# Split weight buffers four instead of three, raw ones eleven instead of thirteen, and the one-hot token columns by eight compares

## The chip, the cores and the metric

The kernel runs on one core of a Trainium2 chip. What counts is the time of one execution on the device, in microseconds (us); of several runs the median is taken. A profile is one execution recorded instruction by instruction. Its engines are TensorE (PE, with its weight loads as PEld), VectorE (DVE), ScalarE (ACT), GpSimd (POOL) and SyncE (SP, which here only issues DMAs). Work reaches an engine in the order of its own queue; engines wait for one another through semaphores.

## The reference, cut to what matters

One layer of a backbone over 1024 latent tokens of width 1024: a normalised input is projected, goes through a long convolution and a gated recurrence, is projected back and added to x. Then comes the part that the change touches, a mixture of 16 experts in which each expert chooses its 128 tokens:

```
aff = softmax(h @ router_w)                      # 1024 x 16
gates, idx = top_k(aff.T, cap)                   # cap = 2 * 1024 / 16 = 128 tokens for each expert
xg = h[idx]                                      # 128 x 1024 per expert
y  = (silu(xg @ w1[e]) * (xg @ w3[e])) @ w2[e]   # w1, w3: 1024 x 2048, w2: 2048 x 1024
out = zeros.at[idx].add(y * gates)               # back to the tokens
```

The result is scaled, added to x and normalised. All is float32.

## The kernel before, in words

The matrix products keep float32 accuracy by splitting each operand into a high half (a rounded copy) and a low half (the rest): `mm3` (L63) makes three matmuls, high by high, high by low, low by high.

The expert weights, 402 MB, are read once, in 384 pieces of 1 MB (128 partitions x 2048 float32). Each expert is worked in two halves of 1024 hidden columns, `i` in 0 to 31. A half takes four pieces of w1, four of w3 and then, for the half before it, four of w2 (`order`, L977). A piece goes through these stages:

- `fetch(n)` (L986) issues its load, on SP's queue, into a buffer `raw`. There are NA = 8 of these in one pool and NB = 5 in another, used in turn. The first eight pieces are loaded during the output projection, by POOL (`stored`, L1035), the next five by POOL right after it (L1112).
- `split(n)` (L1212) copies `raw` to `ehi` on ACT (L1217) and subtracts it into `elo` on DVE (L1223). There are NHI = 3 buffers of each. The first three low halves are made by POOL instead (L1221). When the low half is done the `raw` buffer is free for another load.
- `take()` (L1243) hands the next split piece to PE and, just before, orders the split and the load of later ones: `split(at + NHI - 1)` and `fetch(at + NHI - 1 + NA + NB)`. With that, up to NHI + NA + NB = 16 pieces are loaded or on their way.
- PE multiplies it: 12 matmuls of 128x512 per piece, into `pa` (w1, w3) or `pb` (w2).

Between these stand the other jobs of a half: `sa` is the activation, on ACT (L1280) and DVE (L1282); it is transposed by PE (L1316) and split again into `hh` by ACT (L1318) and DVE (L1319). Once per expert the result is scaled on DVE (L1305) and added to the tokens in memory by an indirect DMA of POOL (L1310). Also once per expert, two experts ahead, `gather(e)` (L1179) finds the tokens: `posT` holds for each token its place (1 to 128) in the expert's list, `iot` the numbers 1 to 128; comparing them gives one-hot columns `oh`, and 16 small matmuls with token numbers give the list `idx`, by which POOL loads the rows `xg` (L1191). `transposed` (L1194) turns these to `hcT`, by PE, ACT (`hf`, L1207, and L1208) and DVE (L1209).

The program is written in one order, but a planner lays out each engine's queue by costs and due times of its own, so that for instance the transposes of one half stand among the matmuls of the next. `issue_after` (`after`, L1022) keeps an instruction behind another.

Ahead of the experts come the output projection and the routing (L1083, t = 0 to 9), the search for each expert's threshold in ten rounds (L1128, which use the tables `jcol` and `rmat`), the places `posT` (L1169), the first two gathers and 9 matmuls that nobody reads (`idle`, L1257). The tables `rmat` and `jcol` are loaded into the pool `late`, which opens at L888. The pool `tp` (L1006) lies where the arena of the stages before was, which closes at L958.

Of the kernel before, what the change touches and what calls it, by code (L numbers as in the profile page):

```python
# [11 lines left out]
F32 = mybir.dt.float32  # L12
F32R = mybir.dt.float32r
BF16 = mybir.dt.bfloat16
# [4 lines left out]
ALU = mybir.AluOpType  # L19
# [3 lines left out]
P = 128  # L23
# [4 lines left out]
NE = 16  # L28
# [29 lines left out]
def kernel(ctx: ExitStack, tc: tile.TileContext, T: dict, out: bass.AP, dbg=None, stop=None):  # L58
    nc = tc.nc
    V, S, PE, G = nc.vector, nc.scalar, nc.tensor, nc.gpsimd  # L60
# [7 lines left out]
    def f32(a):  # L68
        return a.bitcast(F32)

    def brow(src, off, n):

        return bass.AP(tensor=src.tensor, offset=src.offset + off, ap=[[0, P], [1, n]])
# [4 lines left out]
    def bank(tag, bufs, shape=(P, 512), dtype=F32):  # L78
        return ps.tile(list(shape), dtype, tag=tag, bufs=bufs, name=tag)
# [25 lines left out]
    pad = lambda pool, n: pool.tile([P, n], F32, name="pad")  # L105
# [550 lines left out]
    if True:  # L656
# [4 lines left out]
        for hd in range(4):  # L661
# [71 lines left out]
            for dr in range(2):  # L733
                seq = [8, 9] + list(range(7)) if dr == 0 else [9, 8] + list(range(7, 0, -1))
                prev = None
                for b in range(3):
# [9 lines left out]
                    for i, c in enumerate(grp):  # L746
                        n = 3 * b + i
# [139 lines left out]

    late = ctx.enter_context(tc.tile_pool(name="late", bufs=1))  # L888
    aff = late.tile([P, 8, NE], F32, name="aff")
    posT = late.tile([P, 8, NE], BF16, name="posT")  # L890
    iot = late.tile([P, P], BF16, name="iot")
    nc.gpsimd.dma_start(iot, T["iota"])
    tok = late.tile([P, 8, 2], BF16, name="tok")
    nc.gpsimd.dma_start(tok, T["tok"])
    pad(late, 40)
    rmat = late.tile([P, 3, P], BF16, name="rmat")
    nc.gpsimd.dma_start(rmat, T["rmat"])
    jcol = late.tile([P, 10], F32, name="jcol")
    nc.scalar.dma_start(jcol, T["jcol"])
    octx = ctx.enter_context(ExitStack())  # L900
    op = octx.enter_context(tc.tile_pool(name="op", bufs=1))
    pad(op, 112)
# [70 lines left out]


    NS = 2 * NE
    NA, NB, NHI = 8, 5, 3
    order = []  # L977
    for i in range(NS + 1):
        if i < NS:
# [6 lines left out]
    def fetch(n, eng=nc.sync):  # L986


        last = n - NP
        if last < 5:  # L990
            nm, i, j = order[n] if last < 0 else ("x", 0, last)
            e, fc = divmod(i, 2)
            if last == 4:
                src = brow(T["final_g"], 0, D).rearrange("p (a n) -> p a n", a=1)
            elif nm == "x":
                src = xacc[2 * j * P:2 * (j + 1) * P, :].rearrange("(c p) n -> p c n", p=P)
            elif nm == "exp_w2":
                src = T[nm][e].rearrange("(q c p) n -> q p c n", p=P, c=2)[4 * fc + j]
            else:
                src = T[nm][e].rearrange("(k p) f -> p k f", p=P)[:, 2 * j:2 * j + 2, fc * 1024:(fc + 1) * 1024]  # L1000
            early = n % (NA + NB) < NA
            raws[n] = (ew if early else eb).tile([P, 2048], F32, name="raw", bufs=NA if early else NB)
            return eng.dma_start(raws[n].rearrange("p (a b) -> p a b", b=1024)[:, 0:src.shape[1], :], src)

    tctx = ctx.enter_context(ExitStack())
    tp = tctx.enter_context(tc.tile_pool(name="tp", bufs=1, side="right"))  # L1006
    R = tp.tile([P, L], F32, name="R")


    rwg = tp.tile([P, 8, 32], F32, name="rwg")  # L1010
# [11 lines left out]
    def after(ins):  # L1022
        return tc.issue_after(ins.ins if hasattr(ins, "ins") else ins)
# [49 lines left out]
    def rows8(t):  # L1073
        h2, st = tl[t]["h2"], tl[t]["st"]
        pa = bank("pb", 2)
        PE.transpose(pa[:, 0:P], tl[t]["a8"].rearrange("p e j -> p (e j)"), ident)
        tl[t]["row"] = S.copy(R[:, t * P:(t + 1) * P], pa[:, 0:P])
        V.tensor_copy(aff[:, t, :], tl[t]["a8"][:, :, 0])
# [49 lines left out]
    for r in range(10):  # L1128
        V.tensor_scalar(junk, R, thr.bitcast(F32), None, ALU.is_ge, ALU.add, accum_out=cnt)
        V.tensor_scalar(ind, cnt, float(CAP), None, ALU.is_ge)  # L1130
# [48 lines left out]
    def gather(e):  # L1179

        oh = ep.tile([P, 8, P], BF16, name="oh", bufs=1)
        V.tensor_tensor(oh, iot[:].unsqueeze(1).broadcast_to([P, 8, P]), posT[:, :, e:e + 1].broadcast_to([P, 8, P]), ALU.is_equal)
        pi = bank("pt", 2)
        for a in range(8):
            for i in range(2):
                PE.matmul(pi[:, 0:1], oh[:, a, :], tok[:, a, i:i + 1], start=(a + i == 0), stop=(a + i == 8))
        idx = ep.tile([P, 1], I32, name="idx", bufs=4)
        f_ = V.tensor_copy(idx, pi[:, 0:1])
        found[0] = found[0] or f_
        xg = ep.tile([P, D + NE], F32, name="xg", bufs=3)  # L1190
        G.indirect_dma_start(xg[:], None, h2d[:], bass.IndirectOffsetOnAxis(ap=idx[:, 0:1], axis=0))  # L1191
        return idx, xg

    def transposed(e, xg):  # L1194
        xT = [a[:, :, e % 2 * P:(e % 2 + 1) * P] for a in hcT]
        for b in range(2):
            pt = bank("pt", 2)
            hf = ep.tile([P, 4, P], F32, name="hf", bufs=2)
            for c in range(4):
                k = 4 * b + c  # L1200
                PE.transpose(pt[:, c * P:(c + 1) * P], xg[:, k * P:(k + 1) * P], ident)
            for c in range(4):
                k = 4 * b + c
                if e == 0 and b == 1:
                    V.tensor_scalar(hf[:, c, :], pt[:, c * P:(c + 1) * P], gs2[:, k:k + 1], mod2[:, k, 0:1], ALU.mult, ALU.add)
                else:
                    S.activation(hf[:, c, :], pt[:, c * P:(c + 1) * P], AF.Identity, scale=gs2[:, k:k + 1], bias=mod2[:, k, 0:1])  # L1207
            S.copy(xT[0][:, 4 * b:4 * b + 4, :], hf)  # L1208
            V.tensor_tensor(xT[1][:, 4 * b:4 * b + 4, :], hf, f32(xT[0][:, 4 * b:4 * b + 4, :]), ALU.subtract)  # L1209
        return xT  # L1210

    def split(n):  # L1212
        if n < NP:
            raw = raws.pop(n)
            hi = eb.tile([P, 2048], F32R, name="ehi", bufs=NHI)
            with after(tl[7]["row"]):
                S.copy(hi, raw)  # L1217
            lo = eb.tile([P, 2048], F32R, name="elo", bufs=NHI)
            if n < NHI:
                with after(pieces[-1]):  # L1220
                    pieces.append(G.tensor_tensor(lo, raw, f32(hi[:]), ALU.subtract))  # L1221
            else:
                V.tensor_tensor(lo, raw, f32(hi[:]), ALU.subtract)  # L1223
            parts[n] = [t.rearrange("p (a b) -> p a b", b=1024) for t in (hi, lo)]
# [18 lines left out]
    def take():  # L1243
        nonlocal at
        if at > 0:
            split(at + NHI - 1)
            fetch(at + NHI - 1 + NA + NB)
        at += 1
        return parts.pop(at - 1)

    for n in range(NHI):
        split(n)
        fetch(n + NA + NB)
    g = {0: gather(0)}
    g[1] = gather(1)

    idle = bank("pb", 2)  # L1257
    for _ in range(9):
        PE.matmul(idle[:, 0:P], ident, ident, start=True, stop=True)
    xTs = {0: transposed(0, g[0][1])}  # L1260
    py = None
    hs_ = {}
    for i in range(NS + 1):
        e, fc = divmod(i, 2)
# [46 lines left out]
        if i < NS:  # L1311
            hh = [ep.tile([P, 8, P], F32R, name=f"hh{i_}") for i_ in range(2)]
            for b in range(2):
                pt = bank("pt", 2)
                for c in range(4):
                    PE.transpose(pt[:, c * P:(c + 1) * P], sa[:, b, c * P:(c + 1) * P], ident)  # L1316
                pv = pt.rearrange("p (c t) -> p c t", t=P)
                S.copy(hh[0][:, 4 * b:4 * b + 4, :], pv)  # L1318
                V.tensor_tensor(hh[1][:, 4 * b:4 * b + 4, :], pv, f32(hh[0][:, 4 * b:4 * b + 4, :]), ALU.subtract)  # L1319
            hs_[i] = hh  # L1320
            if fc == 0:
                if e + 2 < NE:
                    g[e + 2] = gather(e + 2)
                if e + 1 < NE:
                    xTs[e + 1] = transposed(e + 1, g[e + 1][1])
# [152 lines left out]
```

## Time and profile before

| | |
|---|---|
| runs shown | 2187.92, 2191.95, 2196.3 us; median 2191.95 |
| profiled execution | 2189.24 us, of which the span from first to last instruction 2186.7 |
| PE | 2048.9 us busy, 94% of the span |
| DVE | 1733.5 us, 79% |
| ACT | 1242.2 us, 57% |
| POOL | 201.7 us, 9% |
| low halves `elo` on DVE (L1223) | 863.3 us in 381 |
| high halves `ehi` on ACT (L1217) | 732.8 us in 384 |
| DMA | 565.94 MB, mean 259 GB/s |

A busy PE is not a PE at its peak: matmuls overlap, and their ends are modelled (398 ns stand for one, while they start closer together). So lost time is read from the starts, or from what the weight loads wait for. Idle time of an engine that is not the bottleneck costs nothing. In a row of waits the engine and line that waited stand first, then what ended the wait; the releaser is inferred.

### The profile page before, as it was taken

The numbers are of one execution on the slowest core, as the hardware profiler recorded it, in microseconds if no ns is written. First come the engines' busy times: TensorE is split into PE (matmuls) and PEld (weight loads), VectorE is DVE, ScalarE is ACT, GpSimd is POOL, SyncE is SP. The second block draws the span as 40 slices with busy tenths as digits, with TensorE's granted clock in tenths as the row PEclk, the third lists the DMA queues.
The fourth block names the chain that finished last, engine by engine and source line by source line (L and its number), as shares of the span: only waits on it lengthen the run. The fifth ranks groups of instructions, "written<-read, shape, count | busy, mean of one in ns | idle before, by whom it ended". The sixth has DMA issues, their size and how long they took to land.

```text
span 2186.7 us, 30384 instructions
## 1 busy us (share of the span) xinstructions
PE 2048.9 (94%) x11761; PEld 1621.4 (74%) x11761; DVE 1733.5 (79%) x2051; ACT 1242.2 (57%) x1461; POOL 201.7 (9%) x234
## 2 busy tenths in 40 slices
PE   7987899799999998894999999999999999999997
PEld 2444788788788786773888888787877878787775
DVE  6778356746778887666899999888988889888887
ACT  3566235333542212142877777777777777777774
POOL 1121100100000002124000000000000000100000
PEclk9998999899999999996999999999999999999999
DMA  7874521320234327476999999999999999999992
GB/s 246 271 260 149 159 64 54 108 83 21 64 112 144 111 88 256 141 256 248 343 372 379 397 387 369 358 384 373 381 363 360 387 381 362 364 381 375 352 332 120
DMA packets 185404, 565.94 MB, mean 259 GB/s; under 512 B 15545, under 2 KB 26380, under 8 KB 185261
## 3 DMA queue, kind: packets, MB, share of 16 engines
q1 hardware_dynamic: 147044, 478.41, 58.9%
q0 software_dynamic: 28784, 76.46, 11.5%
q10 hardware_dynamic: 9432, 9.15, 1.3%
q8 instruction: 92, 1.51, 0.3%
q14 instruction: 52, 0.42, 0.1%
HBM read 522.59 MB, written 41.50 MB: 258 GB/s over the span
## 4 chain that ended last, share of the span: by engine, by line
PE 76%; DVE 9%; issue 5%; DMA 5%; ACT 4%; POOL 1%; DVEq 0%; ACTq 0%; SPq 0%; POOLq 0%
PE pa L65 15%; PE pa L66 15%; PE pa L64 14%; PE pb L66 5%; PE pb L65 5%; PE pb L64 5%; PE pt L864 2%; PE pb L845 2%; DVE elo L1223 2%; PE pf L546 2%; ACT ehi L1217 2%; PE pt L1316 1%; DVE arena L727 1%; DVE arena L725 1%; DMA oraw<-in_w_out 1%
## 5 line engine op out<-in xcount | busy, mean ns | idle before, releaser
L1223 DVE TENSOR_TENSOR elo<-raw,ehi 128x2048 fp32r<-128x2048 f32 x381 | 863.3, 2289 | 103.3 <-ACT ehi L1217 99.4
L1217 ACT CAST ehi<-raw 128x2048 fp32r<-128x2048 f32 x384 | 732.8, 1917 | 213.6 <-PE pb L66 93.8
L65 PE MATMUL pa<-elo,hcT 128*128 128x512 f32 x1024 | 407.6, 398 | 14.7 <-DVE elo L1223 14.6
L66 PE MATMUL pa<-ehi,hcT 128*128 128x512 f32 x1024 | 401.6, 392 | 0.0
L64 PE MATMUL pa<-ehi,hcT 128*128 128x512 f32 x1024 | 377.0, 392 | 2.0 <-ACT hcT L1208 1.4
L65 PEld LDWEIGHTS pa<-elo,hcT 128*128 128x128 f32 x1024 | 193.0, 188 | 72.5 <-DVE elo L1223 34.3
L64 PEld LDWEIGHTS pa<-ehi,hcT 128*128 128x128 f32 x1024 | 192.9, 189 | 42.5 <-ACT hcT L1208 1.8
L66 PEld LDWEIGHTS pa<-ehi,hcT 128*128 128x128 f32 x1024 | 193.2, 189 | 37.5
L65 PE MATMUL pb<-elo,hh 128*128 128x512 f32 x512 | 204.9, 400 | 0.0
L66 PE MATMUL pb<-ehi,hh 128*128 128x512 f32 x512 | 200.0, 391 | 0.4 <-DVE hh L1319 0.4
L64 PE MATMUL pb<-ehi,hh 128*128 128x512 f32 x512 | 184.6, 390 | 0.4 <-ACT hh L1318 0.4
L66 PE MATMUL pa<-hT,wlo 128*128 128x512 f32 x448 | 177.6, 397 | 0.5 <-DVE wlo L580 0.5
L64 PE MATMUL pa<-hT,whi 128*128 128x512 f32 x448 | 177.9, 397 | 0.0
L65 PE MATMUL pa<-hT,whi 128*128 128x512 f32 x448 | 175.8, 393 | 0.0
L1310 POOL DMA_INDIRECT xacc<-xg,idx x15 | 45.4, 3024 | 846.2 <-DVE xg L1305 846.2
L64 PEld LDWEIGHTS pb<-ehi,hh 128*128 128x128 f32 x512 | 96.1, 188 | 21.6 <-ACT hh L1318 0.9
L65 PEld LDWEIGHTS pb<-elo,hh 128*128 128x128 f32 x512 | 96.1, 188 | 21.5
L66 PEld LDWEIGHTS pb<-ehi,hh 128*128 128x128 f32 x512 | 96.2, 188 | 18.8 <-DVE hh L1319 0.9
L66 PEld LDWEIGHTS pa<-hT,wlo 128*128 128x128 f32 x448 | 84.1, 188 | 18.7 <-DVE wlo L580 1.4
L65 PEld LDWEIGHTS pa<-hT,whi 128*128 128x128 f32 x448 | 84.2, 188 | 16.9 <-issue 0.2
L64 PEld LDWEIGHTS pa<-hT,whi 128*128 128x128 f32 x448 | 84.2, 188 | 16.8 <-issue 0.2
L546 PE MATMUL pf<-Yh,mt 128*128 128x256 f32 x256 | 73.8, 421 | 16.8 <-ACT he L552 5.9
(407 smaller groups left out, 3112.1 us busy)
## 6 DMA issues: line engine op xcount, KB each, us to landing
raw<-in_exp_w SPq DMA_DIRECT2D x371, 1024.0 KB, 7.7
aw<-in_ada_w SPq DMA_DIRECT2D x96, 256.0 KB, 4.9
wraw<-in_w_in SPq DMA_DIRECT2D x64, 256.0 KB, 3.3
raw<-in_exp_w POOLq DMA_DIRECT2D x13, 1024.0 KB, 8.3
mt<-in_fwm POOLq DMA_DIRECT2D x64, 128.0 KB, 3.6
Hd<-he ACTq DMA_DIRECT2D x32, 256.0 KB, 4.4
wod<-arena POOLq DMA_DIRECT2D x32, 256.0 KB, 3.5
arena<-in_fwm SPq DMA_DIRECT2D x32, 256.0 KB, 7.6
```

The costliest lines, as they stand in the source:

```text
L64: PE.matmul(ps, lhs[0], rhs[0], start=first, stop=False)
L65: PE.matmul(ps, lhs[0], rhs[1], start=False, stop=False)
L66: PE.matmul(ps, lhs[1], rhs[0], start=False, stop=last)
L546: PE.matmul(pt[:, :HC], mt[:, i, :], Y[:, 2 * n + i, :], start=(i == 0), stop=(i == 1))
L725: V.tensor_tensor(kv, kv, view(F2, h, [[2 * h, nb], [LT - h, 2], [0, h]]), ALU.mult)
L727: V.tensor_tensor(qv, qv, view(F2, LT + h, [[2 * h, nq], [-(LT + h), 2], [0, h]]), ALU.mult)
L845: PE.matmul(px[:, j, :], fm[:, j, i, :], Y[:, 2 * n + i, :], start=(i == 0), stop=(i == 1))
L864: PE.matmul(pz[:, j, :], im[:, i, j, :], pp[:, i, :], start=(i == 0), stop=(i == 1))
L1217: S.copy(hi, raw)
L1223: V.tensor_tensor(lo, raw, f32(hi[:]), ALU.subtract)
L1310: G.indirect_dma_start(xacc[:], bass.IndirectOffsetOnAxis(ap=idx[:, 0:1], axis=0), xg[:, 0:D], None, compute_op=ALU.add)
L1316: PE.transpose(pt[:, c * P:(c + 1) * P], sa[:, b, c * P:(c + 1) * P], ident)
```

## The change

The raw buffers of the second pool go from 5 to 3 (11 in all) and the split pairs from 3 to 4. In bytes the pool stays the same: two raw buffers are 16 KB per partition, one split pair as well. The look-ahead goes from 16 pieces to 15. The first three splits stay with POOL; the fourth is ordered after the first expert's tokens are transposed, with ACT and DVE.

The compare of `iot` with `posT`, one instruction over 128x1024 with two broadcast inputs, becomes eight over 128x128, each with a column of `posT` as a scalar operand. For that `posT` becomes float32. The tables `rmat` and `jcol` move from `late` to `tp`, and so their loads come later in the program.

```
-    posT = late.tile([P, 8, NE], BF16, name="posT")
+    posT = late.tile([P, 8, NE], F32, name="posT")
...
-    pad(late, 40)
-    rmat = late.tile([P, 3, P], BF16, name="rmat")
-    nc.gpsimd.dma_start(rmat, T["rmat"])
-    jcol = late.tile([P, 10], F32, name="jcol")
-    nc.scalar.dma_start(jcol, T["jcol"])
+    pad(late, 50)
...
-    NA, NB, NHI = 8, 5, 3
+    NA, NB, NHI = 8, 3, 4
...
     R = tp.tile([P, L], F32, name="R")
+    rmat = tp.tile([P, 3, P], BF16, name="rmat")
+    nc.gpsimd.dma_start(rmat, T["rmat"])
+    jcol = tp.tile([P, 10], F32, name="jcol")
+    nc.scalar.dma_start(jcol, T["jcol"])
...
         oh = ep.tile([P, 8, P], BF16, name="oh", bufs=1)
-        V.tensor_tensor(oh, iot[:].unsqueeze(1).broadcast_to([P, 8, P]), posT[:, :, e:e + 1].broadcast_to([P, 8, P]), ALU.is_equal)
+        for a in range(8):
+            V.tensor_scalar(oh[:, a, :], iot, posT[:, a, e:e + 1], None, ALU.is_equal)
...
-            if n < NHI:
+            if n < 3:
                 with after(pieces[-1]):
                     pieces.append(G.tensor_tensor(lo, raw, f32(hi[:]), ALU.subtract))
...
-    for n in range(NHI):
+    for n in range(3):
         split(n)
         fetch(n + NA + NB)
...
     xTs = {0: transposed(0, g[0][1])}
+    for n in range(3, NHI):
+        split(n)
+        fetch(n + NA + NB)
```

## Rows read from the trace of the kernel before

**Rows 1.** The page: busy us of each engine (share of the span), instructions.
```profile
PE 2048.9 (94%) x11761; PEld 1621.4 (74%) x11761; DVE 1733.5 (79%) x2051; ACT 1242.2 (57%) x1461; POOL 201.7 (9%) x234
```
**Rows 2.** Waits, 1030 to 2190 us: who <- released by: us in total, times, longest.
```profile
ACT ehi L1217 <- PE pb L66: 93.8, 91, 1.6
...
PEld pa L65 <- DVE elo L1223: 34.3, 60, 2.0
```
**Rows 3.** Groups of instructions, 1050 to 2190 us: busy us, mean ns, idle before.
```profile
L1223 DVE TENSOR_TENSOR elo<-raw,ehi 128x2048 fp32r<-128x2048 f32 x377 | 854.2, 2289 | 95.1 <-ACT ehi L1217 91.2
L1217 ACT CAST ehi<-raw 128x2048 fp32r<-128x2048 f32 x376 | 717.9, 1918 | 207.7 <-PE pb L66 93.8 <-PE pa L66 82.9 <-DVE sa L1282 24.2
```
**Rows 4.** Timeline of PE about 1519 us: start us, us, instruction.
```profile
1519.31 0.39 PE L66 MATMUL pa<-ehi,hcT 128*128 128x512 f32 x1
...
1519.99 0.39 PE L66 MATMUL pa<-ehi,hcT 128*128 128x512 f32 x1
```
**Rows 5.** Waits of the weight loads, 1140 to 1340, then 1340 to 2060 us.
```profile
PEld pa L65 <- DVE elo L1223: 0.4, 2, 0.2
...
PEld pa L65 <- DVE elo L1223: 27.4, 50, 2.0
PEld L1186 <- DVE hh L1319: 2.5, 9, 0.3
```
**Rows 6.** Timeline of DVE about four compares, four experts.
```profile
1201.73 1.22 DVE L1182 TENSOR_TENSOR oh<-iot,posT 128x1024 bf16<-128x1024 bf16 x1
...
1270.25 1.22 DVE L1182 TENSOR_TENSOR oh<-iot,posT 128x1024 bf16<-128x1024 bf16 x1
...
1477.79 1.22 DVE L1182 TENSOR_TENSOR oh<-iot,posT 128x1024 bf16<-128x1024 bf16 x1
...
1546.16 2.29 DVE L1223 TENSOR_TENSOR elo<-raw,ehi 128x2048 fp32r<-128x2048 f32 x1
1548.37 1.22 DVE L1182 TENSOR_TENSOR oh<-iot,posT 128x1024 bf16<-128x1024 bf16 x1
```
**Rows 7.** Two windows: length, PE, PEld, DVE, ACT, POOL busy, clock, DMA share, GB/s.
```profile
1140.00:1340.00 200.00, 200.00 (x960) 165.46 (x958) 181.82 (x110) 154.08 (x121) 10.57 (x6) 1.00 1.00 381
1340.00:2060.00 720.00, 708.18 (x3312) 572.99 (x3312) 637.46 (x385) 540.42 (x428) 53.07 (x20) 1.00 0.99 372
```
**Rows 8.** Waits of SP's queue from 900 us, and the page's DMA issues.
```profile
SPq L1003 <- DVE elo L1223: 943.2, 370, 27.6
...
raw<-in_exp_w SPq DMA_DIRECT2D x371, 1024.0 KB, 7.7
```
**Rows 9.** PE's timeline about 2045 us, and the window behind it.
```profile
2044.55 0.39 PE L66 MATMUL pa<-ehi,hcT 128*128 128x512 f32 x1
...
2047.79 0.80 PE L65 MATMUL pa<-elo,hcT 128*128 128x512 f32 x1 [1.59 <-DVE elo L1223]
...
2048.00:2051.00 3.00, 3.00 (x8) 2.33 (x9) 3.00 (x3) 1.53 (x1) 0.00 (x0) 0.51 0.98 358
```
**Rows 10.** Waits of the weight loads, 1030 to 1140, then 2060 to 2160 us.
```profile
PEld pa L65 <- DVE elo L1223: 1.4, 3, 0.7
...
PEld pa L65 <- DVE elo L1223: 5.2, 5, 1.4
PEld pb L66 <- DVE hh L1319: 0.9, 1, 0.9
```
**Rows 11.** A window at the start of the experts, columns as in rows 7.
```profile
1030.00:1040.00 10.00, 9.97 (x36) 8.11 (x37) 4.12 (x4) 4.43 (x3) 0.00 (x0) 0.81 0.01 2
```
**Rows 12.** DVE's timeline at 2125 us, and the instructions of L1130.
```profile
2125.37 1.66 DVE L1268 TENSOR_SCALAR hcT<-iot,idf 128x128 fp32r<-128x128 bf16 x8
...
L1130 DVE TENSOR_SCALAR ind<-cnt x10: 146/150/157, 994.5 to 1013.0; 128x1 bf16<-128x1 f32 x10
```
**Rows 13.** Timelines of PE and of DVE ahead of the first gather.
```profile
1016.67 3.88 PE L1259 MATMUL pb<-ident 128*128 128x128 f32 x18
...
1017.51 1.23 DVE L1182 TENSOR_TENSOR oh<-iot,posT 128x1024 bf16<-128x1024 bf16 x1
```
**Rows 14.** Timelines of POOL and of ACT where the arena comes free.
```profile
937.21 0.57 POOL L1036 DMA_DIRECT2D xacc<-oxt  x1 [10.04 <-DVE oxt L1029]
...
930.96 0.63 ACT L1033 ACTIVATE oh<-oxt 128x512 f32<-128x512 f32 x1 [0.87 <-DVE oxt L1029]
```

## The prediction

> **What bounds the kernel now.** I read the page's busy times first: TensorE (PE) 94% of the span, VectorE (DVE) 79% [rows 1]. In the expert stage, the second half of the span, the DMA engines are full too (a share of 0.99 to 1.00 [rows 7]), so three things could set its pace. The waits between 1030 and 2190 us tell them apart. PE waits for one thing that counts: the low half of a split weight piece, `elo`, written by DVE at L1223. Its weight loads sat idle 34.3 us in 60 such waits. ScalarE (ACT) in turn waits for PE before it may write the high half `ehi`, 93.8 us behind the matmuls into `pb` alone: the three pairs of split buffers are all in use [rows 2]. That is a ring: PE frees a pair, ACT fills `ehi` (1.92 us), DVE fills `elo` (2.29 us) [rows 3], 4.2 us in a row, while PE has two pieces left, each 12 matmuls at about 0.227 us (1519.31 to 1519.99 is three) [rows 4], so 5.4 us. The slack is 1.2 us, and any other instruction of that length on ACT or DVE ahead of a split shows on PE.
>
> Whether it does varies along the stage. From 1140 to 1340 us PE lost 0.4 us to `elo`; from 1340 to 2060 us it lost 27.4 [rows 5]. The one-hot compare, once per expert, stood 68.5 us apart in the first stretch (1201.73 to 1270.25) and 70.6 in the second (1477.79 to 1548.37) [rows 6]. So an expert costs PE 68.5 us where nothing holds it, and that is the floor that I use. DVE was 91% busy in the fast stretch (181.8 of 200) and 89% in the slow one, so it is not DVE's throughput, but the order of its work and the short ring [rows 7].
>
> Loads are not the bound. The DMA queue waits for split pieces, 943.2 us in 370 waits, and a 1 MB load lands 7.7 us after its issue [rows 8]. DMA moved 381 GB/s in the fast stretch and 372 in the slow one: it follows the demand [rows 7].
>
> **The change part by part.**
>
> *Fourth pair of split buffers.* The split of piece n+4 now stands where that of n+3 stood, and waits for the same release by PE. So every `elo` is written one place of the queue earlier with respect to its use, at least 2.2 us (the time for which a low half holds DVE, 1546.16 to 1548.37 [rows 6]), usually one PE piece, 2.7 us. No wait in the trace is longer than 2.0 us [rows 2], so each is covered. What they cost, stretch by stretch: from 1340 to 2040 us there are 9.9 experts of 70.6 us, each 2.06 above the floor, 20.4 us [rows 6]. At 2045 us several waits pile up: from 2044.55 to 2047.79 PE starts three matmuls, 0.68 us of work, so 2.6 us are lost; then its granted clock is 0.51, which is 1.2 GHz, after these 3 us with hardly any matmul, and only eight start in the next 3 us where 13 fit, 1.2 us; together 3.8 [rows 9]. Before 1140 us PE lost 1.4 us, after 2060 us 5.2 [rows 10]. In all 20.4 + 3.8 + 1.4 + 5.2 = 30.8 us. The idle time of the weight loads, 34.3 us [rows 2], is somewhat more, since it holds the ordinary gap before a load as well.
>
> Not all of it will come. The order of work on each engine is laid out by a planner with costs of its own, so the new kernel has a new order; and when `elo` is in time, the next late thing is `hh`: 2.5 us in 9 waits [rows 5] and 1.8 in two of 0.9 near the end, of which one stands in [rows 10]. I keep nine tenths of 30.8: **28 us**. The bounds are 0 (a new order that puts as much back) and 34.3 + 2.5 + 1.8 = 39 us.
>
> *Two raw buffers fewer.* The look-ahead is 15 pieces in place of 16. A buffer is refilled when its split ends, and its own split comes 11 pieces later: 11 x 2.85 us (68.5 / 24) less the 4.2 of the split is 27 us, against 7.7 for a landing. Cost 0. It would cost if loads took over 27 us. At the start the DMA engines come to rest because all buffers are full (a share of 0.01 in 1030 to 1040 us [rows 11]); one piece less is in hand then, and PE reaches it some 14 pieces, 40 us, later. POOL issues three loads instead of five before its three splits, which so begin earlier, off the chain.
>
> *Eight compares for one.* One 128x1024 compare takes 1.22 us; instructions overlap by 0.08 (the low half of 1546.16 takes 2.29 and the next starts after 2.21), so it holds DVE for 1.14 [rows 6]. No row has a 128x128 compare from bfloat16 to bfloat16. The nearest is L1268, the same input with a wider output: eight in 1.66 us, which hold DVE for 1.58. From below, a 128x1 one takes 0.15, and with the same overlap that is 0.07 x 8 = 0.6 us [rows 12]. So one gather costs DVE between 0.5 us less and 0.44 more; I take 0.2 more, nearer L1268, 3 us in 16 gathers. It lies on an engine that is idle 9% of 68.5 us, 6 us per expert, with PE now one piece further from it: 0 on the path. Without that cover it is at most 0.44 x 16 = 7 us.
>
> The Trainium skill speaks against this edit: "VectorE: DVE Perf Modes", in the section on the TRN2 errata, says that each VectorE instruction pays a fixed latency, so that many small tiles pay it many times, and advises 512 elements or more. By its measured 150 cycles and its fourfold rate for a single-source bfloat16 operation, eight would take an estimated 8 x 182 / 0.96 GHz = 1.5 us, 0.3 more than now. L1268 comes to 1.58 [rows 12], so the trace agrees on the side; by either, the sum stays.
>
> In the first gather the compares are on the chain to the first expert matmul; but there PE is busy with 18 warm-up matmuls until 1020.55, past the end of the compare at 1018.74 [rows 13], and then come the index, an indirect load and the transposes. Eight compares end by 1019.2 at the most: no loss. If the gather's matmuls now come ahead of the warm-up, 1.6 us are gained. I count 0.
>
> *The fourth split ahead of the loop.* It comes after the first transposes, where ACT and DVE wait. Done before the loop it helps with the 1.4 us before 1140 us, counted above. Put ahead of `hf` in ACT's and DVE's queues, it would cost up to 4.2 us once; I count 0.
>
> *`rmat` and `jcol` later.* One DMA issue on POOL and one on ACT go from the place where `late` opens to the one where the arena comes free, about 929 us. POOL is idle there for 10.0 us before 937.2, ACT for 0.9 before 930.96 [rows 14]. On POOL the issue stands ahead of the stores of `xacc`, on ACT ahead of the squares of L1033, and it waits for transposes that those need anyway; the tables are needed only by the search of thresholds, more than 50 us on. Cost 0, at worst 0.9 us. `posT` in float32 has as many elements: 0.
>
> *Sum.* The profiled execution took 2189.2 us (span 2186.7). Less 28 it is 2161. The median of the runs shown, 2191.95, is 2.7 above it, so I predict **2164 us**.
>
> **The rivals.**
>
> *Half comes back* (2172 to 2184). The planner uses the room to set splits ahead of other work on ACT and DVE, and waits for `hh` or `sa` take the place of half of those for `elo`: 2192 - 14 = 2178. For it: the present order lost nothing for three experts and 2 us per expert for ten [rows 5, 6]. Against: ACT's splits still wait for PE's release, so none can run further ahead than today.
>
> *Nothing moves* (2186 to 2198). The loads take PE's place, as 11 buffers must serve a faster ring. For it: DMA share 0.99. Against: 381 GB/s and landings in time at the pace of 68.5 us [rows 7, 8]; that pace needs 25.2 MB / 68.5 us = 367. It would be so if a load took over 27 us.
>
> *Slower: the switch between experts.* The pile-up of 2045 us, where DVE waits for an `ehi` that stands behind `hf` and `hcT` on ACT, comes at every switch in the new order. Its price there is 3.8 us with the slow clock [rows 9]. At 15 switches that is 57, less the 31 gained: 2192 + 26 = 2218. From 9 switches on it is slower. Against: one more piece is split when a switch begins, 2.7 us, which covers the stall of 2.6 in the same order.
>
> **How the numbers follow.** The forecast (2154 to 2172) gets 0.70; half comes back 0.15, of which 0.10 lie below 2181; nothing moves 0.07; slower 0.08. What a measurement can tell from no change is 0.5%, 11 us: faster means under 2181. So faster 0.80, same 0.12, slower 0.08. The range is 2152 (the bound of 39 and 1 of the 1.6 us of the start, from 2192) to 2186, with some 0.13 outside.
>
> **What would show it.** If right: waits of weight loads for `elo` fall from 34.3 to under 6 us; compares stand 68.5 us apart throughout; the DMA queue still waits for splits, and ACT's wait for PE stays above 150 us; L1182 becomes groups of eight in 1.0 to 1.6 us; the first expert matmul starts within 2 us of 1030. Wrong: ACT waiting for `raw` loads, PE waiting for `hh`, `sa` or `hcT` by more than 10 us, or granted clock near 0.5 at the switches.

## The result, and the profile after

The changed kernel takes **2215.99 us** (median of 4 runs, 2209.56 to 2218.02), the kernel before 2189.93 on the same chip (4 runs, 2185.81 to 2196.3). The ratio is 1.0115, interval 1.0098 to 1.0131: slower by some 26 us, where 2164 was forecast. The span of the profiled execution grew from 2186.7 to 2212.9 us.

PE is busy for about as long as before [rows 1], over a longer span:

```profile
PE 2056.4 (93%) x11761; PEld 1626.0 (73%) x11761; DVE 1729.2 (78%) x2163; ACT 1232.6 (56%) x1461; POOL 209.4 (9%) x232
```

The same two windows as [rows 7]. The first, with 0.4 us of waits before, is still almost full; the second has lost 19 us of PE's work, and the DMA engines have slowed with it (356 GB/s in place of 372):

```profile
1140.00:1340.00 200.00, 198.74 (x952) 164.03 (x951) 176.71 (x129) 148.56 (x119) 18.62 (x6) 1.00 0.99 372
1340.00:2060.00 720.00, 689.42 (x3184) 555.63 (x3185) 609.29 (x424) 512.38 (x406) 48.65 (x19) 0.99 0.97 356
```

Waits from 1030 to 2190 us, as [rows 2] (who, released by: us in total, times, longest):

```profile
ACT ehi L1218 <- PE pb L66: 67.1, 68, 1.6
...
PEld pa L65 <- DVE elo L1224: 46.4, 45, 2.0
ACT ehi L1218 <- PE pa L66: 46.2, 60, 4.2
ACT hf L1208 <- PE pt L1202: 35.0, 12, 3.2
...
PEld pa L64 <- ACT ehi L1218: 9.6, 10, 1.0
```

ACT waits less for a free pair (67.1 and 46.2 us; before, 93.8 behind `pb` [rows 2] and 88.7 behind `pa`), so the fourth pair is in use. But PE's weight loads wait longer for `elo`, 46.4 us against 34.3, in fewer waits; they now wait for `ehi` too, ten times; and ACT stands 35.0 us ahead of `hf`, once per expert and 3.2 us at most. The kernel before, in the same window:

```profile
ACT hf L1207 <- PE pt L1201: 9.6, 11, 1.8
```

The index of a gather, `idx`, is written once per expert; its instructions give the pace of the experts in the slow part (first and last start; ten instructions, nine experts). The line of the kernel before comes first:

```profile
L1188 DVE CAST idx<-pt x10: 157/159/161, 1334.4 to 1969.6; 128x1 int32<-128x1 f32 x10
```

```profile
L1189 DVE CAST idx<-pt x10: 147/148/150, 1333.5 to 1997.5; 128x1 int32<-128x1 f32 x10
```

That is 70.6 us per expert before and 73.8 after (664.0 us by nine): 3.2 us more, 29 us in these nine, and 3.3 in the one ahead of them (72.5 after 69.2), 32 in ten. The loss sits here, and some 6 us are less elsewhere. The first expert matmul starts at 1027.22, 2.8 us before the 1030 of the kernel before; that isn't shown to be the change's, for in a run below whose program is that of the kernel before up to there (the silu behind the split) it starts at 1027.08.

**One switch.** VectorE's timeline about 1550 us of the changed kernel (start, us, instruction, idle before it):

```profile
1548.29 2.28 DVE L1224 TENSOR_TENSOR elo<-raw,ehi 128x2048 fp32r<-128x2048 f32 x1
1550.49 0.68 DVE L1323 TENSOR_TENSOR hh<-pt,hh 128x512 fp32r<-128x512 f32 x1
1551.09 2.28 DVE L1224 TENSOR_TENSOR elo<-raw,ehi 128x2048 fp32r<-128x2048 f32 x1
1553.29 0.68 DVE L1323 TENSOR_TENSOR hh<-pt,hh 128x512 fp32r<-128x512 f32 x1
1553.89 0.15 DVE L1189 CAST idx<-pt 128x1 int32<-128x1 f32 x1
```

An `elo` stands between the two `hh`. The kernel before, at the same switch:

```profile
1544.53 1.28 DVE L1319 TENSOR_TENSOR hh<-pt,hh 128x512 fp32r<-128x512 f32 x2
1546.08 0.16 DVE L1188 CAST idx<-pt 128x1 int32<-128x1 f32 x1 [0.27 <-PE pt L1186]
```

Each `hh` and `idx` read a bank of `pt`, of which there are two, used in turn. So TensorE can't make the first four transposes of the next tokens (L1202) before the second `hh` is done, nor the last four before `idx` is. Here all eight stand behind both:

```profile
1554.66 1.04 PE L1202 MATMUL pt<-ident,xg 128*128 128x128 f32 x8
```

TensorE isn't idle ahead of them: the planner has put other matmuls there, so the delay lies in the order of TensorE's queue too. ScalarE at the same switch:

```profile
1548.36 3.72 ACT L1218 CAST ehi<-raw 128x2048 fp32r<-128x2048 f32 x2
1555.30 1.85 ACT L1208 ACTIVATE hf<-pt,mod,gs 128x128 f32<-128x128 f32 x5 [3.23 <-PE pt L1202]
...
1557.53 1.18 ACT L1208 ACTIVATE hf<-pt,mod,gs 128x128 f32<-128x128 f32 x3
1558.57 1.93 ACT L1218 CAST ehi<-raw 128x2048 fp32r<-128x2048 f32 x1
```

ScalarE does nothing for 3.23 us, while a split stands behind `hf`. TensorE then comes to that split's piece:

```profile
1559.63 0.39 PE L66 MATMUL pa<-ehi,hcT 128*128 128x512 f32 x1
1560.56 0.73 PE L64 MATMUL pa<-ehi,hcT 128*128 128x512 f32 x2 [0.54 <-ACT ehi L1218]
1562.88 0.50 PE L65 MATMUL pa<-elo,hcT 128*128 128x512 f32 x1 [1.59 <-DVE elo L1224]
...
1563.52 0.63 PE L65 MATMUL pa<-elo,hcT 128*128 128x512 f32 x1
1563.94 0.63 PE L66 MATMUL pa<-ehi,hcT 128*128 128x512 f32 x1
...
1566.86 0.62 PE L64 MATMUL pa<-ehi,hcT 128*128 128x512 f32 x2
```

From 1559.63 to 1566.86 it starts 13 matmuls, 2.95 us of work at 0.227, and so loses 4.3 us. Behind the stall they start 0.43 us apart: the window 1563.5 to 1566.5 has a granted clock of 0.50, which is 1.2 GHz, as the one behind the pile-up of [rows 9] had. The two waits are those of that pile-up as well (0.52 and 1.59 us there). In the kernel before it stands at 2045 us alone; in the changed kernel between 1340 and 2010 us it stands at ten switches.

```profile
1563.50:1566.50 3.00, 3.00 (x8) 2.30 (x7) 3.00 (x2) 3.00 (x4) 2.98 (x1) 0.50 0.84 274
```

### The profile page after: what moved, and what is told of

It reads as the page before. It is cut to its first block, busy times and chain, and to the rows that moved or that the text cites. A ratio compares the mean times of both kernels' runs of the same rounds, so it can differ in the third digit from the quotient of the medians.

```text
span 2212.9 us, 30500 instructions
## 1 busy us (share of the span) xinstructions
PE 2056.4 (93%) x11761; PEld 1626.0 (73%) x11761; DVE 1729.2 (78%) x2163; ACT 1232.6 (56%) x1461; POOL 209.4 (9%) x232
## 4 chain that ended last, share of the span: by engine, by line
PE 69%; issue 10%; DVE 9%; DMA 6%; ACT 5%; POOL 1%; DVEq 0%; POOLq 0%; ACTq 0%; SPq 0%
PE pa L65 13%; PE pa L66 13%; PE pa L64 12%; PE pb L65 5%; PE pb L64 5%; PE pb L66 5%; DVE elo L1224 3%; ACT ehi L1218 2%; PE pb L845 2%; PE pt L864 2%; PE pf L546 2%; ACT hf L1208 1%; PE pt L1320 1%; DMA raw<-in_exp_w 1%; DMA oraw<-in_w_out 1%
## 5 line engine op out<-in xcount | busy, mean ns | idle before, releaser
L1218 ACT CAST ehi<-raw 128x2048 fp32r<-128x2048 f32 x384 | 723.3, 1918 | 133.0 <-PE pb L66 67.1
L65 PEld LDWEIGHTS pa<-elo,hcT 128*128 128x128 f32 x1024 | 194.8, 190 | 85.7 <-DVE elo L1224 46.4
L546 PE MATMUL pf<-Yh,mt 128*128 128x256 f32 x256 | 72.5, 416 | 18.4 <-ACT he L552 6.6
```

Of the source, the lines that this page charges most:

```text
L65: PE.matmul(ps, lhs[0], rhs[1], start=False, stop=False)
L546: PE.matmul(pt[:, :HC], mt[:, i, :], Y[:, 2 * n + i, :], start=(i == 0), stop=(i == 1))
```

## The experiments

My theory: with four pairs the split at the last take of a half is that of piece n+3, not n+2, so one `elo` more is written ahead of `hh` in the program's text; the planner puts it ahead of the second `hh` on VectorE; transposes, `hf`, the next split and TensorE follow late. Rivals: the eight compares, the eleven raws, or four pairs that are slower in themselves (memory traffic).

**Compares alone** (`NB, NHI` back to 5, 3; the rest of the change stays).

```
-    NA, NB, NHI = 8, 3, 4
+    NA, NB, NHI = 8, 5, 3
```

Expected: 

> The changed kernel with three pairs of split buffers and thirteen raws again, so that of the change the eight compares, the 32-bit posT and the moved rmat and jcol are left. Theory 'one remainder ahead of hh' (the fourth pair let the planner put one elo of each switch on VectorE ahead of the second hh and of idx, so the transposes of the next tokens, hf on ScalarE and the split behind it come 2.3 us or more later): 2190 us, ratio 1.000 within 0.002, and at a switch VectorE runs hh, hh, idx, elo, as in the kernel before. Rival 'compares' (eight small compares between the remainders on VectorE make it late): the whole loss or most of it, 2210 to 2216.

Measured: 2189.21 us, ratio 0.9997 (0.9984 to 1.001). The compares, the float32 `posT` and the moved tables together cost nothing.

**Pairs and raws alone** (the wide compare and the 16-bit `posT` back).

```
-        for a in range(8):
-            V.tensor_scalar(oh[:, a, :], iot, posT[:, a, e:e + 1], None, ALU.is_equal)
+        V.tensor_tensor(oh, iot[:].unsqueeze(1).broadcast_to([P, 8, P]), posT[:, :, e:e + 1].broadcast_to([P, 8, P]), ALU.is_equal)
```

Expected: 

> The changed kernel with the one wide compare and the 16-bit posT of before: four pairs, eleven raws. Theory 'one remainder ahead of hh': 2214 to 2218, ratio 1.011 to 1.013, and VectorE runs hh, elo, hh at the switches from the fifth expert on. Rival 'compares': 2190. Rival 'raws' (eleven raws leave the loads late): 2216 too, so this run tells that one apart only by its waits: splits would then wait for loads, and the DMA would show as what ended the idle time before ehi.

Measured: 2220.78 us, ratio 1.0139 (1.0109 to 1.017): the whole loss, a little above what I expected.

**Raws alone** (the kernel of the last run with `NHI` 3).

```
-    NA, NB, NHI = 8, 3, 4
+    NA, NB, NHI = 8, 3, 3
```

Expected: 

> Eleven raws with three pairs and the wide compare: the one part of the change that no run so far shows by itself. Theory 'one remainder ahead of hh': the raws have no part in it, 2190, ratio 1.000 within 0.003. Rival 'raws' (two raws fewer leave loads late, or let the planner write a worse order): 2200 or more, with a split that waits for its load, or hh, elo, hh on VectorE.

Measured: 2188.86 us, ratio 1.0001 (0.9988 to 1.0014). So it is the fourth pair.

**One `elo` later** (the changed kernel; pairs, raws and compares stay).

```
+            elif n == held[0]:
+                held[1] = lambda: V.tensor_tensor(lo, raw, f32(hi[:]), ALU.subtract)
...
             for c in range(8):
                 if c % 2 == 0:
+                    held[0] = at + NHI - 1 if c == 6 and i < NS else -1
                     w = take()
...
             if fc == 0:
                 if e + 2 < NE:
                     g[e + 2] = gather(e + 2)
+                if held[1]:
+                    held[1]()
+                    held[1] = None
```

Expected: 

> The changed kernel with nothing altered but the place in the text of one elo in twelve pieces: the remainder that is split at the last take of a half is written behind hh (and behind the gather, where there is one) and not ahead. Theory 'one remainder ahead of hh': VectorE runs hh, hh, idx, elo again, ScalarE waits 0.8 us instead of 3.2 for the transposes at a switch, and of the 26 us some 18 come back: 2198 (2194 to 2203); what stays is what the new order of the rest is worth. Rivals 'raws', 'compares' and 'memory' (four pairs take SBUF bandwidth or keep VectorE fuller): none of them is touched, 2216.

Measured: 2187.25 us, ratio 1.0000 (0.9985 to 1.0016). One instruction in twelve splits, written some lines later, gives back all of the loss: 25 us by the two ratios (1.0115 and 1.0000), 28.7 from median to median (which were not measured side by side). I had expected 18, from the two orders and the durations in the trace without the slow clock behind a stall. VectorE at a switch of this run (the held remainder is L1226), and the pace of its experts, 70.7 us:

```profile
1541.12 1.28 DVE L1329 TENSOR_TENSOR hh<-pt,hh 128x512 fp32r<-128x512 f32 x2
1542.67 0.16 DVE L1189 CAST idx<-pt 128x1 int32<-128x1 f32 x1 [0.27 <-PE pt L1187]
1542.75 2.29 DVE L1226 TENSOR_TENSOR elo<-raw,ehi 128x2048 fp32r<-128x2048 f32 x1
```

```profile
L1189 DVE CAST idx<-pt x10: 157/158/160, 1330.6 to 1966.9; 128x1 int32<-128x1 f32 x10
```

ScalarE's `hf` follows the first `hh` by 2.56 us here (1541.12 to 1543.68), by 4.81 in the changed kernel (1550.49 to 1555.30). The 2.25 us between are the one `elo`, which holds VectorE for 2.20. ScalarE's row:

```profile
1543.68 1.86 ACT L1208 ACTIVATE hf<-pt,mod,gs 128x128 f32<-128x128 f32 x5 [0.97 <-PE pt L1202]
```

**Between `hh` and `idx`** (the same edit, but the three lines stand ahead of `if fc == 0`).

```
             hs_[i] = hh
+            if held[1]:
+                held[1]()
+                held[1] = None
             if fc == 0:
```

Expected: 

> As the run in which one elo of a half is written behind hh and the gather (2187), but written between the two: behind hh, ahead of idx. It parts the two steps by which the early remainder does harm. Theory: the second hh gives a bank of pt free 2.3 us earlier than in the changed kernel, which returns the larger part, and idx, whose bank the second block of transposes wants, still waits 2.3 us behind the remainder, which keeps the smaller: 2200 (2195 to 2206). Rival 'hh alone': all of it is back, 2188. Rival 'idx alone': nothing, 2216.

Measured: 2194.97 us, ratio 1.0025 (1.0011 to 1.0038), at the lower bound of the range. Its order and its pace:

```profile
1546.97 1.28 DVE L1329 TENSOR_TENSOR hh<-pt,hh 128x512 fp32r<-128x512 f32 x2
1548.17 2.28 DVE L1226 TENSOR_TENSOR elo<-raw,ehi 128x2048 fp32r<-128x2048 f32 x1
1550.37 0.15 DVE L1189 CAST idx<-pt 128x1 int32<-128x1 f32 x1
```

```profile
L1189 DVE CAST idx<-pt x10: 148/150/151, 1336.0 to 1979.3; 128x1 int32<-128x1 f32 x10
```

71.5 us per expert: of the 3.1 us between 73.8 and 70.7, 2.3 hang on the second `hh` and 0.8 on `idx`. The slow clock counts among the 2.3, since this run doesn't have it from 1340 to 2010 us. Neither rival fits.

**The order alone** (the kernel before, three pairs).

```
-        if at > 0:
-            split(at + NHI - 1)
-            fetch(at + NHI - 1 + NA + NB)
...
+    def refill(k):
+        if k % 2 == 1:
+            split(at + NHI - 1)
+            fetch(at + NHI - 1 + NA + NB)
...
+                    refill(k)
...
+                refill(c)
```

Expected: 

> The kernel before with three pairs, thirteen raws and the wide compare; only the call that splits and fetches is written behind the matmuls of a piece instead of ahead of those of the next, so that the last split of a half stands ahead of hh in the text, as with four pairs. Theory 'one remainder ahead of hh': as slow as the changed kernel without any part of the change, 2210 (2204 to 2218), with hh, elo, hh on VectorE at the switches. Rivals 'raws', 'compares', 'memory': 2190, ratio 1.000.

Measured: 2220.93 us, ratio 1.0144 (1.0118 to 1.017), above my range and as slow as the pairs and raws alone. No buffer, load or compare differs from the kernel before. (The last split of the gate's and of the up's pieces moves in the text as well, ahead of the silu and of the product; the run can't part that from `hh`.) VectorE at its switch:

```profile
1557.10 0.68 DVE L1323 TENSOR_TENSOR hh<-pt,hh 128x512 fp32r<-128x512 f32 x1
1557.70 2.28 DVE L1223 TENSOR_TENSOR elo<-raw,ehi 128x2048 fp32r<-128x2048 f32 x1
1559.90 0.68 DVE L1323 TENSOR_TENSOR hh<-pt,hh 128x512 fp32r<-128x512 f32 x1
```

Its experts follow each other by 73.8 us, as in the changed kernel:

```profile
L1188 DVE CAST idx<-pt x10: 145/148/151, 1339.7 to 2004.2; 128x1 int32<-128x1 f32 x10
```

That says where the 26 us came from, and not where the forecast gain of 28 went. Two pairs of runs take that up.

**The silu behind the split** (the kernel before; one edge).

```
-                S.copy(hi, raw)
+                his.append(S.copy(hi, raw))
...
-                        silu = S.activation(sa[:, h, :], pab[h], AF.Silu)
+                        with after(his[-1]):
+                            silu = S.activation(sa[:, h, :], pab[h], AF.Silu)
```

The reason for it, in the changed kernel's ScalarE rows: a silu waits 4.23 us for TensorE ahead of a split, and TensorE then waits for that split.

```profile
1587.70 5.52 ACT L1218 CAST ehi<-raw 128x2048 fp32r<-128x2048 f32 x3
1597.45 0.60 ACT L1284 ACTIVATE sa<-pa 128x512 f32<-128x512 f32 x1 [4.23 <-PE pa L66]
1597.94 1.90 ACT L1218 CAST ehi<-raw 128x2048 fp32r<-128x2048 f32 x1
```

```profile
1602.22 0.50 PE L65 MATMUL pa<-elo,hcT 128*128 128x512 f32 x1 [0.95 <-DVE elo L1224]
```

The kernel before has the same order there, a silu that waits ahead of a split:

```profile
1587.62 0.60 ACT L1280 ACTIVATE sa<-pa 128x512 f32<-128x512 f32 x1 [2.84 <-PE pa L66]
1588.11 1.90 ACT L1217 CAST ehi<-raw 128x2048 fp32r<-128x2048 f32 x1
```

Expected: 

> The kernel before with one edge on ScalarE: the silu of a half is put behind the newest split's ehi. In the traces of both kernels the silu of every even half stands ahead of a split, waits there for TensorE, and the remainder of that split is 1.3 to 1.4 us late. Theory 'order of the queues': eleven or so of these stalls go, some 15 us: 2175 (2170 to 2180), ratio 0.993. Rival 'release': the split waits for its buffer anyway, 2190. Rival 'late silu': sa and so hh come later, and it is slower, 2195 or more.

Measured: 2171.07 us, ratio 0.9922 (0.9903 to 0.9942), faster than both kernels. From 1340 to 2010 us TensorE no longer stops for `elo`; the kernel before had nine such waits there, 8.6 us in all. Its row shows 69.3 us per expert, 1.3 less than before:

```profile
L1188 DVE CAST idx<-pt x10: 157/158/161, 1331.6 to 1955.5; 128x1 int32<-128x1 f32 x10
```

**Four pairs with both mended** (the edit of one `elo` later and this edge, in the changed kernel).

```
+                held[1] = lambda: V.tensor_tensor(lo, raw, f32(hi[:]), ALU.subtract)
...
+                        with after(his[-1]):
+                            silu = S.activation(sa[:, h, :], pab[h], AF.Silu)
```

Expected: 

> The changed kernel with one elo of a half written behind hh and the gather, and the silu behind the newest ehi: four pairs with both of the found orders mended. Theory 'order of the queues': hf and hcT still stand ahead of the split that the fourth pair could take, so the fourth pair is worth nothing beyond three pairs with the silu mended: 2172 (2168 to 2178). Rival 'the fourth pair pays once its queue is mended', as the prediction had it: nearly all waits for elo go, 2160 or less.

Measured: 2169.94 us, ratio 0.9917 (0.9898 to 0.9936). The two intervals overlap, the medians are 1.1 us apart: the fourth pair adds nothing that can be told. Weight loads from 1340 to 2060 us, with three pairs and then with four:

```profile
PEld pa L65 <- DVE elo L1225: 13.2, 40, 2.0
```

```profile
PEld pa L65 <- DVE elo L1230: 13.8, 32, 2.0
```

Both are half of the 27.4 us of [rows 5], and neither pair count has the advantage.

**Half of each later load left out**, with four pairs and with three. Every expert piece from the seventeenth on loads 512 of 1024 columns.

```
+            cut = 512 if 16 <= n < NP else 1024
+            return eng.dma_start(raws[n].rearrange("p (a b) -> p a b", b=1024)[:, 0:src.shape[1], 0:cut], src[:, :, 0:cut])
...
+                raw4 = raw.rearrange("p (a b) -> p a b", b=1024)[:, :, 0:512].unsqueeze(2).broadcast_to([P, 2, 2, 512])
```

Expected, four pairs: 

> The changed kernel with half of every weight load from piece 16 on left out: 512 of each 1024 columns are loaded, and the split reads the loaded half twice, so that its instructions keep their size; the products are computed from those columns. Theory 'the order is laid out as if the loads set the pace' (from the fifth expert on the planner has hh and hf come early between the splits because it expects the next raw late): with lighter loads all experts get the order that the first four have, 68.5 us each, 2167 (2160 to 2172), as fast as three pairs with light loads; ScalarE runs two splits more ahead of hh at a switch. Rival 'four pairs are slower in themselves': 2190 or more, over 71 us for an expert.

Expected, three pairs: 

> The kernel before with the same half of the later weight loads left out. Theory 'the order is laid out as if the loads set the pace': 68.5 us for every expert, 2166 (2160 to 2172): the pair count makes no difference where the order is that of the first experts. Rival 'the fourth pair pays', as the prediction had it for the present order: three pairs still wait for elo, 70 us for an expert, some 2185.

Measured: 2160.97 us with four pairs, ratio 0.9875 (0.9859 to 0.9892), and 2164.32 with three, 0.9895 (0.9877 to 0.9913); the intervals overlap, the medians are 3.4 us apart. The experts follow each other by 68.5 us in both:

```profile
L1190 DVE CAST idx<-pt x10: 157/159/159, 1332.2 to 1948.7; 128x1 int32<-128x1 f32 x10
```

```profile
L1189 DVE CAST idx<-pt x10: 157/159/159, 1333.2 to 1950.1; 128x1 int32<-128x1 f32 x10
```

ScalarE at a switch, with four pairs. Counted along ScalarE's queue, the `hh` of the eighth expert's first half stands behind the split of piece 179, where the changed kernel has it behind 177, and `hf` behind 180 in place of 179; one split is left between them, and `hf` waits for nothing.

```profile
1535.27 1.07 ACT L1329 CAST hh<-pt 128x512 fp32r<-128x512 f32 x2
1537.08 1.92 ACT L1223 CAST ehi<-raw 128x2048 fp32r<-128x2048 f32 x1 [0.73 <-PE pa L66]
1538.89 1.85 ACT L1209 ACTIVATE hf<-pt,mod,gs 128x128 f32<-128x128 f32 x5
```

The order that the first experts have lasts to the end when the loads are light. That fits a planner that expects the next raw late and fills the gap with `hh`, `hf` and silu; but the loads on the chip are lighter too, so these two runs alone don't part the planner's view of the loads from the loads. Why the planner sets one `elo` between the two `hh` from the fifth expert on stays open. With full loads and other orders 69.3 us was reached, so at most the last 0.8 us of an expert could be the loads' own.

## Why the prediction was wrong

**The step that failed** is the one on the fourth pair: "The split of piece n+4 now stands where that of n+3 stood, and waits for the same release by PE. So every `elo` is written one place of the queue earlier". One place earlier in the text puts one `elo` per half ahead of `hh`, and on VectorE it got ahead of the second `hh` and of `idx`. I counted who waits for `elo` and not who waits behind it. The text named the planner's new order and gave it a tenth of the gain. At a switch the step fails on ScalarE as well: counted along its queue, the `hh` of the eighth expert's first half stands behind the split of piece 177 and `hf` behind that of 179, in the kernel before and in the changed one. So the split that TensorE waits for there came no place earlier. Between switches the pair was used: from 1340 to 2010 us 132 of 219 splits start before TensorE has begun the last matmul of the piece three back, and in the kernel before none of 228 does. That paid nothing, and the waits for `elo` rose to 46.4 us, where under 6 were forecast.

**The 30.8 us were not the price of a missing pair.** Three pairs and four give the same time in both like orders (2171 and 2170; 2164 and 2161). [Rows 2] shows ACT waiting for PE's release, and I read that as a ring too short. But in [rows 5] the same three pairs lose 0.4 us in three experts: that row already said that three pairs are enough in a good order. By the medians of those two pairs of runs a fourth pair was worth 1 to 3 us, which the intervals don't tell from nothing. Some 1.3 us of the 2.1 lost per expert before was a silu in front of a split, which a fourth pair leaves there.

**The rival that won, and by what.** "Slower: the switch between experts" named the right place (a split behind `hf` and `hcT` on ACT, with the slow clock behind it) and the time, 2218. Its sum is right by luck, because its terms are off together: it took 3.8 us at 15 switches, 57, less a gain of 31. The stall came at ten switches, with the slow clock at six of them, and ten experts took 32 us longer than before; there was no gain to set against it, and the 6 us that are less elsewhere make it 26. What I held against it, one more piece split when the switch begins, was in hand only if ScalarE's queue let the split through. The Trainium skill says in "Perfetto Trace Analysis", in its section "Tensor Engine Instruction", that ScalarE and VectorE work their queues strictly in order; the 3.23 us ahead of `hf` agree, with a split behind it.

**What held.** The raws: 0. The compares: nothing on the path; eight take 1.38 us in one row, within the 1.0 to 1.6 forecast.

```profile
1197.60 1.38 DVE L1183 TENSOR_SCALAR oh<-iot,posT 128x128 bf16<-128x128 bf16 x8
```

The Trainium skill speaks against many small compares by a fixed latency for each ("VectorE: DVE Perf Modes", the section on the TRN2 errata). The trace agrees on the side: 1.38 us by this row, and an estimated 1.5 by the page, against 1.22 for the wide one. By the run of the compares it changes no time. The moved tables: 0, as far as the run of the compares, which has them too, can tell. The start was forecast within 2 us of 1030; the first expert matmul comes at 1027.22, just outside:

```profile
1027.22 0.79 PE L64 MATMUL pa<-ehi,hcT 128*128 128x512 f32 x1 [1.44 <-ACT hcT L1209]
```

The signs named for "right" failed: waits for `elo` of 46.4 us, experts 73.8 us apart and not 68.5, and ACT ahead of `ehi` waiting 113 us for PE, not above 150. The signs named for "wrong" came half: a granted clock of 0.50 at six switches, but PE waiting for `elo` itself, late through others, and not for `hh`, `sa` or `hcT`.

## What to carry to other kernels

A wait for a buffer's release doesn't show that a buffer is missing: look for a stretch with as many buffers and no waits, and ask what order differs. Where a planner or a program's text orders in-order queues, moving an instruction one place earlier moves others one place later; for each, list who reads what stands behind it, down to the next shared bank. The remedy may be as small: one edge (`silu` behind a split) gained 18 us here, and one subtraction written later repaid the 26 that came with a fourth pair.

## What the runs showed of the hardware

A stall on TensorE cost more than its waits: behind 0.54 and 1.59 us eight matmuls ran 0.43 us apart at a granted clock of 0.50 before the pace of 0.227 came back, 1.6 us more. Six of the ten switches from 1340 to 2010 us are followed by this: the granted clock is 0.50 in the 3 us from 1416.8, 1563.5, 1710.4, 1785.5, 1932.3 and 2007.4 us. Behind the other four, which have the same two waits, it stays 1.00. An expert with such a stretch is followed by the next after 74.4 or 74.5 us, one without after 72.9 or 73.0: 1.5 us more, as in the working above.

The kernel with one `elo` later has neither the two waits nor such a stretch at these switches, and its granted clock from 1340 to 2060 us is 1.00 (0.99 in the changed one, a row shown above):

```profile
1340.00:2060.00 720.00, 706.26 (x3316) 573.12 (x3315) 632.70 (x440) 533.73 (x427) 114.81 (x20) 1.00 0.99 372
```

Six times 1.5 us, 9 us, is an estimate of what the 18, worked out from durations at full clock, had left out: 27, against a return of 25 to 29.
